# The attention's streamed output projection in another order of products, the last head's steps pinned, and a surcharge on POOL's DMAs in the FFN

## The chip, the core and the metric

The kernel runs on one core of a Trainium2 chip. A core has a matrix engine (PE), a vector engine (DVE), a scalar engine (ACT), a general engine (POOL) and an engine that issues DMAs (SP); each works through a queue of its own in order, and semaphores order them against each other. The metric is the device time of one execution in microseconds, over several runs; one further execution is recorded by the hardware profiler, and its rows are quoted below. PE = matmuls, PEld = weight loads; L73 is a helper line on which most vector operations are recorded, so groups are told apart by the tiles that they write and read.

## The reference

One decoder block in float32, sequence and model width 1024: a mixer, then cross-attention to 256 memory tokens, then a gated FFN of width 2816, each behind an rmsnorm and with a residual, and a last rmsnorm. What the change touches:

```python
def mem_cross_attention(n, m, w_xq, w_xkv, w_xo):
    q = (n @ w_xq).reshape(Bsz, S, 4, 256)
    k, v = jnp.split(m @ w_xkv, 2, axis=-1)
    ...
    p = jax.nn.softmax(s, axis=-1)
    o = jnp.einsum('bhsm,bmhd->bshd', p, v).reshape(Bsz, S, 1024)
    return o @ w_xo

def swiglu(n, w_ffn_in, w_ffn_out):
    g, u = jnp.split(n @ w_ffn_in, 2, axis=-1)
    return (jax.nn.silu(g) * u) @ w_ffn_out
...
h = h + mem_cross_attention(rmsnorm(h), rmsnorm(mem), w_xq, w_xkv, w_xo)
h = h + swiglu(rmsnorm(h), w_ffn_in, w_ffn_out)
```

## The kernel before

Every large product is done by seven block products instead of eight (Strassen in Winograd's form). Their names are those of the right operand: B11, B21 and B22 are blocks as they are, T1 to T4 are sums of blocks. Each operand in float32 is split into a high half (a copy on ACT, L233, into a rounded type) and a low half (a subtraction on DVE, L73), and three matmuls, high with high, high with low, low with high, stand for one (L51). So each product needs an ACT step, a DVE step and, for the sums, more steps on DVE or POOL before PE can begin it.

The stages that matter here follow each other:

1. The attention, class Att: for each of four heads h and two halves j of the rows a `score` (matmuls, then on DVE the maximum and the scaled negative of it, on ACT the exponentials, on DVE the reciprocal of the sum and the multiplication by it, tile pe), a `turn` (PE transposes pe; ACT and DVE split it, tile phl) and a `value` (matmuls, copied by ACT into the rows rq of the next product's right operand).
2. The output projection xo, an object of class Stored: its weights stream in (tiles wr; sums of weight blocks were prepared by POOL's DMAs in the DRAM tensor xos_d), both operands are split (tiles ws), products are taken in the order SEQ, and DVE adds them into tiles wk and ga that hold the residual. A block of the output that is final goes through post_xo: stored to h2_d by SP, scaled by ACT into the rows of the FFN's right operand, and its squares summed for the norm (tiles sq, ssum).
3. The FFN: eleven pairs of Units, gate and up, of 256 columns each. Their right operands are an object of class Operands, B, which `upto` brings on step by step. A Unit's weights (tile raw) are summed on POOL or DVE into sa and, for T3 and B22, in place (raw<-raw, raw<-raw,sa), split into whi and wlo, and used. Outputs are tiles o; gpost multiplies a gate's block by the norm (ssum), applies the silu and multiplies again; upost multiplies gate by up and forms the sums of blocks that the down projection takes, and SP stores them in act_d.
4. Beside the FFN, weight_sums issues DMAs on POOL that build the sums of the down projection's weights in down_d, some of them accumulating.

The order on each engine is not written out. A scheduler orders the instructions by times that it estimates; `ahead` gives priority, and `pinned` keeps an instruction in program order with the others that are pinned. `either(ap)` gives an operation to POOL or DVE, whichever of two meters (DVE.t, POOL.t), which add up estimated durations, says would end it sooner. Slots ("op", "aux", "m", "ga") are pools of buffers; a tile may not be written before its slot's last reader is through.

Of the kernel before, what the change touches and what calls it, by code (L numbers as in the profile page):

```python
# [13 lines left out]
ALU = mybir.AluOpType  # L14
AX = mybir.AxisListType
# [63 lines left out]
def block_kernel(ctx: ExitStack, tc: tile.TileContext, t: dict, out: bass.AP):  # L79
# [398 lines left out]
    def store_rows(dst, func=None):  # L478
# [6 lines left out]
            return post  # L485
        return mk

    def weight_sums(todo):


        jobs = []
        for A, d, n, k0 in todo:
            put = lambda m, d=d, n=n, k0=k0, kn=A.shape[2]: (
                d[(m * n + k0) * P:(m * n + k0 + kn) * P].rearrange("(k p) c -> p k c", p=P))
            q = {(i, j): A[j][:, :, half(i)] for i in range(2) for j in range(2)}
            jobs.append([(put(0), q[1, 0], 0), (put(2), q[0, 0], 0), (put(0), q[1, 1], 1), (put(2), q[1, 0], 1),
                         (put(1), put(0), 0), (put(3), q[0, 1], 0), (put(1), q[0, 0], 1), (put(3), put(1), 1)])
        for step in zip(*jobs):
            for o, a, more in step:
                kn = o.shape[1]  # L500
                for c in (slice(0, kn // 2), slice(kn // 2, kn)) if more and kn > 3 else (slice(0, kn),):
                    if more:
                        pinned(POOL.dma_start(o[:, c], a[:, c], accum_op=ALU.add))
                    else:
                        pinned(POOL.dma_start(o, a))
                    yield

    def w_in_units(c0, n, mk):
# [721 lines left out]
    class Wide:  # L1230
# [59 lines left out]
        def fetch(s, m, kp):  # L1290
# [8 lines left out]
            if x == 5:  # L1299
                s.load("T4")  # L1300

        def prep(s, n, pin=None):
            pin = pin or (lambda x: x)
            while len(s.ops) < min(n, 14):
                m, kp = divmod(len(s.ops), 2)
                name, c = s.SEQ[m], slice(2 * kp, 2 * kp + 2)
                s.load(name)
                x = [slot("op", (P, 2, 2, HALF), F32R, name="ws") for _ in range(2)]
                with ahead():
                    if name in s.COMB:  # L1310
                        f, *q = s.COMB[name]
                        o, a, b = (s.quad(*ij)[:, c] for ij in q)
                        f(DVE, o, a, b)
                    split(s.raw[name][:, c], x[0][:, 0], x[0][:, 1], pin=pin)
                    split(s.quad(*s.RIGHT[name])[:, c], x[1][:, 0], x[1][:, 1], neg=name == "T2", pin=pin)
                if name in ("T1", "T2") and s.PLUS:
                    s.raw[s.SEQ[m + 1]] = s.raw[name]
                    s.plus(s.SEQ[m + 1], 2 * kp)
                s.ops.append(x)

        def evac(s, name, u, p):
            i, j = s.OUT[name]
# [39 lines left out]
    class Stored(Wide):  # L1362
# [13 lines left out]

        def fetch(s, m, kp):
            s.load(*s.SEQ[:m + 3])
            if s.base is not None:
                for ij in {0: ((0, 0), (1, 1)), 2: ((0, 1),), 8: ((1, 0),)}.get(2 * m + kp, ()):  # L1380
                    s.home(*ij)

    class Left:

# [224 lines left out]
    def post_xo(o, h, q, last):  # L1609
# [1 line left out]
        ACT.activation(row_xo(o)[:, half(h)], q, AF.Copy, scale=col("norm_ffn", o))  # L1611
        u_xo_stats.take(h, q)

    xo = Stored(t["w_xo"], post_xo, {"T2": "aux", "B21": "aux", "*": "m"},
                {(0, 0): "m", (1, 1): "aux", (0, 1): "aux", (1, 0): "ga"}, h1_d)
    xo.sums_d = xos_d

    class Att:


        def __init__(s, h, j):
            s.h, s.j = h, j

        def score(s, a2):
            kvh, kvl = kv[s.h][:, 0], kv[s.h][:, 1]
            q = [i_q[2 * s.h + i][:, :, half(s.j)] for i in range(2)]
            if s.j == 1 and a2 == 0:
                pe[s.h] = slot("aux", (P, 2, 4, 256), name="pe")
            s.e = pe[s.h][:, s.j]
            p = acc()  # L1630
            for a in range(2):
                o = p[:, a * 256:(a + 1) * 256]
                c = slice((2 * a2 + a) * P, (2 * a2 + a + 1) * P)
                m = 0
                for i in range(2):
                    for x, y in ((0, kvh), (1, kvh), (0, kvl)):
                        PE.matmul(o, q[i][:, x, c], y[:, i], start=m == 0, stop=m == 5)
                        m += 1
            pv = p.rearrange("p (a m) -> p a m", m=256)
            mx = cp.tile([P, 2], F32, name="mx", tag="mx", bufs=3)  # L1640
            DVE.tensor_reduce(mx, pv, AX.X, ALU.max)
            c0 = 4 * s.j + 2 * a2
            DVE.scalar_tensor_tensor(mx, mx, -1.0, xsc[:, c0:c0 + 2], ALU.mult, ALU.mult)
            sm = cp.tile([P, 2], F32, name="sm", tag="sm", bufs=3)
            for a in range(2):
                ACT.activation(s.e[:, 2 * a2 + a], pv[:, a], AF.Exp, bias=mx[:, a:a + 1],
                               scale=xsc[:, c0 + a:c0 + a + 1], accum_out=sm[:, a:a + 1])
            DVE.reciprocal(sm, sm)
            for a in range(2):
                DVE.tensor_scalar(s.e[:, 2 * a2 + a], s.e[:, 2 * a2 + a], sm[:, a:a + 1], None, ALU.mult)  # L1650

        def turn(s, a2):
            if a2 == 0:
                s.pT = [bank(), bank()]
            for a in range(2):
                c = 2 * a2 + a
                for i in range(2):
                    PE.transpose(s.pT[i][:, c * P:(c + 1) * P], s.e[:, c, i * P:(i + 1) * P], ident)
            if a2 == 1:
                s.p = slot("aux", (P, 2, 2, HALF), F32R, name="phl")  # L1660
                for i in range(2):
                    split(s.pT[i], s.p[:, 0, i], s.p[:, 1, i])

        def value(s):
            kvh, kvl, ph, pl_ = kv[s.h][:, 0], kv[s.h][:, 1], s.p[:, 0], s.p[:, 1]
# [7 lines left out]
                ACT.activation(xo.rows(2 * s.h + i, s.j), p, AF.Copy)  # L1673

    pe = {}
    at = [Att(h, j) for h in range(4) for j in (1, 0)]
    for n in range(len(at) + 2):
        a = at[n] if n < len(at) else None
        b = at[n - 1] if 0 < n <= len(at) else None
        z = at[n - 2] if n > 1 else None  # L1680
        if a and a.j == 1 and a.h < 3:
            load_kv(a.h + 1)
        if a:
            a.score(0)
        if b:
            b.turn(0)
        if z:
            z.value()
        if b:
            b.turn(1)  # L1690
        if a:
            a.score(1)
        if n in (3, 4):
            xo.load(xo.SEQ[n - 3])
        if n in (7, 8):
            xo.prep(n - 6)
# [4 lines left out]
    for u in range(D_FF // 256):  # L1701
# [35 lines left out]
        if u < 2:  # L1737
            gate.e = up.e = DVE
        gu.append([gate, up])
    B = Operands(lambda: Row(row_xo), 4, swap=1, order=("B11", "T1", "B21", "B22", "T2", "T3", "T4"))  # L1740
    for n, _ in enumerate(xo.steps()):
        if n >= 8:
            B.upto(2 * n - 14)
        if n == 11:
            gu[0][0].load()
        if n == 13:
# [128 lines left out]
                          stop=k0 + k == KP - 1 and m == 2, skip_group_check=True)  # L1875

    run(group(gu[0], B, gu[1], order=B.order), (side, 1.0))
    w_down = t["w_ffn_out"].rearrange("(k j p) c -> j p k c", j=2, p=P)
    last_sums = chain(weight_sums([(w_down[:, :, k:min(k + 3, KP)], down_d, KP, k)]) for k in range(0, KP, 3))
    for u in range(1, len(gu)):  # L1880
# [79 lines left out]
```

## Time and profile before

| What | Value |
|---|---|
| runs, us | 1949.55, 1950.52, 1953.47 |
| median of the runs, us | 1950.52 |
| the profiled execution, us | 1952.81 |
| its span, from first to last instruction, us | 1951.1 |
| mean granted PE clock | 0.991 |
| POOL in the profile: busy us, instructions | 538.4, 432 |
| DVE: busy us, instructions | 1383.3, 1962 |
| end of the attention, projection, first FFN pairs | about 1100 to 1420 us of the span |

A row of the timeline has the start, the duration, the engine, the line, the operation, the tiles out<-in with partitions and elements, and how many equal ones follow each other; in brackets is how long the engine was idle just before, and what ended that wait ("issue": nothing that the profile shows). A row of the windows has the busy time of each engine in a stretch. A wait costs time only if the engine that waits is the one that the end depends on.

### The profile page before, as it was taken

How to read it: one execution, taken by the hardware profiler on the slowest of the kernel's cores; microseconds unless marked ns; L12 is line 12 of the kernel's file. 1: busy time of each engine (PE TensorE's matmuls, PEld its weight loads, DVE VectorE, ACT ScalarE, POOL GpSimd, SP SyncE). 2: the span in 40 equal slices, each digit the busy share in tenths (PEclk: the TensorE clock that was granted, in tenths of full speed). 3: DMA queues.
4: the chain of work that ended last, by engine and by line, in shares of the span. 5: the costliest groups of instructions: out<-in, count | busy, mean ns of one | idle time of the engine just before them, and what ended most of it. 6: DMA issues, size and time to landing. Idle time of an engine off the chain costs nothing. (4 is left out here: it accounts for less than half of the span.)

```text
span 1951.1 us, 26054 instructions
## 1 busy us (share of the span) xinstructions
PE 1894.7 (97%) x9632; PEld 1592.5 (82%) x9632; DVE 1383.3 (71%) x1962; ACT 901.3 (46%) x1541; POOL 538.4 (28%) x432
## 2 busy tenths in 40 slices
PE   7999999999999999999999998989799999999998
PEld 7998787888878888788888896878688788888888
DVE  7765879877776764653578777887577777866566
ACT  7534564655543544642247565653233333345243
POOL 0012334345443221001112110235444444330002
PEclk9999999999999999999999998999899999999999
DMA  9433383446563653988665563426565555387463
GB/s 345 139 93 101 130 307 108 155 160 191 167 184 122 198 159 119 363 310 247 169 173 201 145 155 126 137 80 173 146 188 158 145 158 167 89 290 272 161 223 125
DMA packets 242899, 345.23 MB, mean 177 GB/s; under 512 B 16442, under 2 KB 143652, under 8 KB 242772
## 3 DMA queue, kind: packets, MB, share of 16 engines
q1 hardware_dynamic: 223380, 293.23, 44.1%
q0 software_dynamic: 17664, 44.04, 10.8%
q10 hardware_dynamic: 1728, 6.29, 0.8%
q8 instruction: 76, 1.25, 0.3%
q14 instruction: 51, 0.42, 0.1%
HBM read 254.06 MB, written 129.30 MB: 196 GB/s over the span
## 5 line engine op out<-in xcount | busy, mean ns | idle before, releaser
L73 DVE TENSOR_TENSOR wlo<-raw,whi 128x512 fp32r<-128x512 f32 x272 | 241.6, 896 | 95.0 <-ACT whi L233 94.9
L233 ACT ACTIVATE whi<-raw 128x512 fp32r<-128x512 f32 x272 | 169.2, 629 | 243.5 <-PE acc L51 204.3
L73 DVE TENSOR_TENSOR o<-acc,o 128x512 f32<-128x512 f32 x244 | 166.9, 684 | 87.6 <-PE acc L51 84.8
L51 PE MATMUL acc<-hl,wd 128*128 128x512 f32 x768 | 174.7, 389 | 1.5 <-ACT wd L233 1.1
L51 PEld LDWEIGHTS acc<-hl,wd 128*128 128x128 f32 x768 | 143.9, 188 | 32.3 <-ACT wd L233 1.7
L51 PE MATMUL acc<-fs 128*128 128x512 f32 (+1 forms) x792 | 155.7, 355 | 0.1
L51 PEld LDWEIGHTS acc<-fs 128*128 128x128 f32 x792 | 130.7, 189 | 20.7 <-issue 0.5
L51 PE MATMUL acc<-ws 128*128 128x512 f32 x576 | 133.9, 390 | 1.4 <-DVE wk L73 1.1
L51 PEld LDWEIGHTS acc<-ws 128*128 128x128 f32 x576 | 107.7, 188 | 24.5 <-issue 1.5
L73 DVE TENSOR_TENSOR fs<-fr,fs 128x1024 fp32r<-128x1024 f32 (+1 forms) x78 | 93.4, 1225 | 35.8 <-ACT fs L233 35.1
L233 ACT ACTIVATE fs<-fr 128x1024 fp32r<-128x1024 f32 (+1 forms) x78 | 74.5, 984 | 92.0 <-PE bank L51 28.7
L233 ACT ACTIVATE whi<-sa 128x512 fp32r<-128x512 f32 x96 | 59.7, 627 | 99.9 <-PE acc L51 98.7
L51 PE MATMUL bank<-ws 128*128 128x512 f32 x432 | 99.8, 390 | 0.0
L73 POOL TENSOR_TENSOR sa<-raw 128x512 f32<-128x512 f32 x43 | 66.6, 1550 | 119.2 <-DMA raw<-in_w_in_dram 73.5
L73 POOL TENSOR_TENSOR raw<-raw,sa 128x512 f32<-128x512 f32 x35 | 45.4, 1298 | 194.3 <-DVE wlo L73 194.3
L51 PEld LDWEIGHTS bank<-ws 128*128 128x128 f32 x432 | 81.4, 188 | 17.0
L73 POOL TENSOR_TENSOR ssum<-ssum,sq 128x512 f32<-128x512 f32 (+1 forms) x24 | 38.2, 1591 | 196.9 <-ACT sq L525 184.4
L73 DVE TENSOR_TENSOR o<-o,ssum 128x512 f32<-128x512 f32 x67 | 65.9, 984 | 35.4 <-ACT o L1704 34.1
L51 PE MATMUL acc<-T1h,whi 128*128 128x512 f32 x192 | 77.6, 404 | 11.3 <-ACT whi L233 8.7
L51 PE MATMUL acc<-T4h,whi 128*128 128x512 f32 x192 | 76.7, 400 | 2.1 <-DVE o L73 2.0
L51 PE MATMUL acc<-B21h,wlo 128*128 128x512 f32 x192 | 76.3, 399 | 2.3 <-DVE wlo L73 2.3
L51 PE MATMUL acc<-T1h,wlo 128*128 128x512 f32 x192 | 76.4, 398 | 1.9 <-DVE wlo L73 1.9
(421 smaller groups left out, 5110.1 us busy)
## 6 DMA issues: line engine op xcount, KB each, us to landing
raw<-in_w_in_dram SPq DMA_DIRECT2D x26, 1024.0 KB, 5.8
raw<-in_w_ffn_in_dram SPq DMA_DIRECT2D x22, 1024.0 KB, 6.7
act_d<-o SPq DMA_DIRECT2D x77, 256.0 KB, 3.7
fr<-act_d SPq DMA_DIRECT2D x35, 512.0 KB, 5.9
down_d<-in_w_ffn_out_dram POOLq DMA_DIRECT2D x18, 768.0 KB, 7.4
fr<-down_d SPq DMA_DIRECT2D x20, 512.0 KB, 3.8
csb<-cs_d SPq DMA_DIRECT2D x15, 512.0 KB, 4.3
fr<-in_w_ffn_out_dram SPq DMA_DIRECT2D x15, 512.0 KB, 6.7
```

The source lines that it names most:

```text
L51: return s.e.matmul(o, x, y, **kw)
L73: return f(*a, **kw)
L233: pin(ACT.activation(hi, src, AF.Copy))
```

## The change

It has four parts. In the attention the halves are taken in the order (0, 1) instead of (1, 0), and the DVE steps of the last head, h = 3, are pinned. The projection becomes a Kept: its products stand in the order B11, B21, T1, T2, B22, T3, T4 instead of B11, T1, B22, T2, B21, T3, T4; the splits of B21 and T1 (steps 2 to 5) are pinned; all its weights come from one pool of slots; its residual tiles are fetched at other steps; the combination for T3 is made early. FFN operands: B no longer swaps the two column halves and is brought on from the projection's fourth step, B11 first. And once the first FFN pair is done, each DMA step of weight_sums adds 3.0 to POOL's meter.

```diff
+    slower = [0.0]
+
     def weight_sums(todo):
...
                     else:
                         pinned(POOL.dma_start(o, a))
+                    POOL.t += slower[0]
                     yield
...
     run(group(gu[0], B, gu[1], order=B.order), (side, 1.0))
+    slower[0] = 3.0
...
+                at = pin or (pinned if len(s.ops) in s.pins else free)
...
+    class Kept(Stored):
+
+        SEQ, FIRST, pins = Wide.SEQ, Wide.FIRST, (2, 3, 4, 5)
+
+        def fetch(s, m, kp):
+            x = 2 * m + kp
+            s.load(*s.SEQ[:m + 3])
+            for ij in {0: ((0, 0),), 2: ((1, 1),), 4: ((0, 1),), 8: ((1, 0),)}.get(x, ()):
+                s.home(*ij)
+            if x == 5:
+                for c in (slice(0, 2), slice(2, 4)):
+                    s.combine("T3", c, lambda x: x)
+                s.combined = ("T3",)
...
-    xo = Stored(t["w_xo"], post_xo, {"T2": "aux", "B21": "aux", "*": "m"},
-                {(0, 0): "m", (1, 1): "aux", (0, 1): "aux", (1, 0): "ga"}, h1_d)
+    xo = Kept(t["w_xo"], post_xo, {"*": "m"},
+              {(0, 0): "m", (1, 1): "aux", (0, 1): "aux", (1, 0): "ga"}, h1_d)
...
+            s.pin = pinned if h == 3 else lambda x: x
...
-            DVE.tensor_reduce(mx, pv, AX.X, ALU.max)
+            s.pin(DVE.tensor_reduce(mx, pv, AX.X, ALU.max))
...
-                    split(s.pT[i], s.p[:, 0, i], s.p[:, 1, i])
+                    split(s.pT[i], s.p[:, 0, i], s.p[:, 1, i], pin=s.pin)
...
-    at = [Att(h, j) for h in range(4) for j in (1, 0)]
+    at = [Att(h, j) for h in range(4) for j in (0, 1)]
...
-    B = Operands(lambda: Row(row_xo), 4, swap=1, order=("B11", "T1", "B21", "B22", "T2", "T3", "T4"))
+    B = Operands(lambda: Row(row_xo), 4, order=("B11", "T1", "B21", "B22", "T2", "T3", "T4"))
     for n, _ in enumerate(xo.steps()):
-        if n >= 8:
-            B.upto(2 * n - 14)
+        if n >= 4:
+            B.upto(min(n - 3, 4) if n < 10 else min(2 * n - 14, 8))
```

What this does to the order on the engines is seen at three places. The first is DVE at the end of the attention, where the last score's sum is inverted (sm), the probabilities are normalized (pe) and their low half is made (phl), while products of the projection are evacuated (wk) and its operands split (ws) or summed (rq). Before:

```order
L73 RECIPROCAL sm_10490<-sm_10490 128x2
L73 SCALAR_TENSOR_TENSOR wk_10561<-acc_10556,wk_10561 128x512
L73 SCALAR_TENSOR_TENSOR wk_10561<-acc_10557,wk_10561 128x512
L73 TENSOR_TENSOR rq_10138<-rq_10379,rq_10138 128x1024
L73 TENSOR_TENSOR ws_10597<-rq_10138,ws_10597 128x1024
L73 TENSOR_SCALAR pe_10343<-pe_10343,sm_10490 128x256 x2
L73 TENSOR_TENSOR ws_10639<-wr_10559,ws_10639 128x1024
L73 SCALAR_TENSOR_TENSOR wk_10561<-acc_10558,wk_10561 128x512
L73 TENSOR_TENSOR ws_10640<-rq_10379,ws_10640 128x1024
```

and behind these four more of 128x1024 before phl. After, on the same engine at the same place:

```order
L73 RECIPROCAL sm_10490<-sm_10490 128x2
L73 TENSOR_SCALAR pe_10343<-pe_10343,sm_10490 128x256
L73 SCALAR_TENSOR_TENSOR wk_10561<-acc_10556,wk_10561 128x512
L73 TENSOR_SCALAR pe_10343<-pe_10343,sm_10490 128x256
L73 SCALAR_TENSOR_TENSOR wk_10561<-acc_10557,wk_10561 128x512
L73 TENSOR_TENSOR phl_10528<-bank_10502,phl_10528 128x512
L73 TENSOR_TENSOR phl_10528<-bank_10503,phl_10528 128x512
L73 SCALAR_TENSOR_TENSOR wk_10561<-acc_10558,wk_10561 128x512
L73 TENSOR_TENSOR rq_10062<-rq_10062,rq_10138 128x1024
```

All sums and splits of 128x1024 now stand behind phl. The second place is POOL in the second FFN pair (o_11514 and o_11518 are that pair's gate output before and after; raw_11800 and raw_11801 the up weights of the pair behind it). Before:

```order
L73 TENSOR_TENSOR o_11514<-o_11514,ssum_9902 128x512
L73 DMA down_d_83<-in_w_ffn_out_dram 128x3x512
L73 TENSOR_TENSOR o_11514<-o_11514,ssum_9902 128x512
L73 DMA down_d_83<-in_w_ffn_out_dram 128x3x512 x2
L73 DMA down_d_83<-down_d_83 128x3x512
L73 TENSOR_TENSOR sa_11975<-raw_11800 128x512
L73 TENSOR_TENSOR sa_11977<-sa_11975,raw_11800 128x512
L73 TENSOR_TENSOR raw_11800<-raw_11800 128x4x128
```

After, on POOL at the same place:

```order
L73 TENSOR_TENSOR o_11518<-o_11518,ssum_9902 128x512
L73 DMA down_d_83<-in_w_ffn_out_dram 128x3x512 x3
L73 DMA down_d_83<-down_d_83 128x3x512
L73 TENSOR_TENSOR sa_11975<-raw_11801 128x512
L73 TENSOR_TENSOR sa_11977<-sa_11975,raw_11801 128x512
L73 DMA down_d_83<-in_w_ffn_out_dram 128x3x512
```

The last row of before, the T3 step on the weights, and one multiplication have left POOL; the four DMAs stand ahead of the sum sa as they did. The third place is DVE in the same pair, at the splits wlo of the up unit's T3, B22 and T4 weights (raw_11513) and the evacuations of its products (o<-acc). After, DVE has:

```order
L73 TENSOR_TENSOR wlo_11746<-raw_11513,whi_11745 128x512
L73 TENSOR_TENSOR o_11664<-acc_11709,o_11664 128x512
L73 TENSOR_TENSOR wlo_11766<-raw_11513,whi_11765 128x512
L73 TENSOR_TENSOR raw_11801<-raw_11801 128x4x128
L73 TENSOR_TENSOR wlo_11785<-raw_11513,whi_11784 128x512
L73 TENSOR_TENSOR o_11518<-o_11518,o_11664 128x512
L73 TENSOR_TENSOR o_11664<-acc_11691,o_11664 128x512
```

The same rows stood there before, but for the fourth: the T3 step on the next pair's up weights has come to DVE, between the splits for B22 and for T4.

More of the change, by code (lines that the diff above doesn't have):

```diff
@@ L1300, in fetch @@
                 s.load("T4")
+        pins = ()
+        combined = ()
         def prep(s, n, pin=None):
-            pin = pin or (lambda x: x)
+            free = lambda x: x
             while len(s.ops) < min(n, 14):
@@ L1309, in prep @@
                 with ahead():
[L1310 to L1315, printed above, removed]
+                    if name in s.COMB and name not in s.combined:
+                        s.combine(name, c, at if s.pins else free)
+                    split(s.raw[name][:, c], x[0][:, 0], x[0][:, 1], pin=at)
+                    split(s.quad(*s.RIGHT[name])[:, c], x[1][:, 0], x[1][:, 1], neg=name == "T2", pin=at)
                 if name in ("T1", "T2") and s.PLUS:
@@ L1319, in prep, with combine @@
                 s.ops.append(x)
+        def combine(s, name, c, pin):
+            f, *q = s.COMB[name]
+            o, a, b = (s.quad(*ij)[:, c] for ij in q)
+            pin(f(DVE, o, a, b))
         def evac(s, name, u, p):
@@ L1378, in fetch @@
             s.load(*s.SEQ[:m + 3])
-            if s.base is not None:
-                for ij in {0: ((0, 0), (1, 1)), 2: ((0, 1),), 8: ((1, 0),)}.get(2 * m + kp, ()):
-                    s.home(*ij)
+    class Kept(Stored):
[9 more added lines that the diff above has]
+                s.combined = ("T3",)
     class Left:
@@ L1626, in score @@
             q = [i_q[2 * s.h + i][:, :, half(s.j)] for i in range(2)]
-            if s.j == 1 and a2 == 0:
+            if s.j == 0 and a2 == 0:
                 pe[s.h] = slot("aux", (P, 2, 4, 256), name="pe")
@@ L1640, in score @@
             mx = cp.tile([P, 2], F32, name="mx", tag="mx", bufs=3)
-            DVE.tensor_reduce(mx, pv, AX.X, ALU.max)
+            s.pin(DVE.tensor_reduce(mx, pv, AX.X, ALU.max))
             c0 = 4 * s.j + 2 * a2
-            DVE.scalar_tensor_tensor(mx, mx, -1.0, xsc[:, c0:c0 + 2], ALU.mult, ALU.mult)
+            s.pin(DVE.scalar_tensor_tensor(mx, mx, -1.0, xsc[:, c0:c0 + 2], ALU.mult, ALU.mult))
             sm = cp.tile([P, 2], F32, name="sm", tag="sm", bufs=3)
@@ L1647, in score @@
                                scale=xsc[:, c0 + a:c0 + a + 1], accum_out=sm[:, a:a + 1])
-            DVE.reciprocal(sm, sm)
+            s.pin(DVE.reciprocal(sm, sm))
             for a in range(2):
-                DVE.tensor_scalar(s.e[:, 2 * a2 + a], s.e[:, 2 * a2 + a], sm[:, a:a + 1], None, ALU.mult)
+                s.pin(DVE.tensor_scalar(s.e[:, 2 * a2 + a], s.e[:, 2 * a2 + a], sm[:, a:a + 1], None, ALU.mult))
         def turn(s, a2):
@@ L1680, in block_kernel @@
         z = at[n - 2] if n > 1 else None
-        if a and a.j == 1 and a.h < 3:
+        if a and a.j == 0 and a.h < 3:
             load_kv(a.h + 1)
```

## The prediction

> **What bounds the kernel now.** I read the page's engine table first, then windows over the stretch that the change touches, then PE's waits there, and last the rows of single engines around each wait. A windows row has start and end, length, then busy time and (instructions) of PE, PEld, DVE, ACT, POOL, the granted clock, the DMA share and GB/s.
>
> ```profile
> PE 1894.7 (97%) x9632; PEld 1592.5 (82%) x9632; DVE 1383.3 (71%) x1962; ACT 901.3 (46%) x1541; POOL 538.4 (28%) x432
> ```
>
> ```profile
> 1190.00:1210.00 20.00, 12.68 (x46) 9.29 (x45) 15.68 (x18) 8.15 (x11) 0.00 (x0) 0.74 0.39 126
> 1250.00:1300.00 50.00, 43.35 (x179) 33.92 (x177) 49.65 (x74) 33.02 (x58) 13.87 (x10) 0.93 0.35 117
> 1350.00:1400.00 50.00, 39.71 (x166) 31.68 (x165) 27.71 (x36) 12.88 (x22) 20.02 (x16) 0.92 0.65 161
> 1390.00:1410.00 20.00, 13.74 (x48) 10.68 (x49) 11.49 (x15) 5.69 (x10) 9.58 (x7) 0.74 0.41 88
> 1500.00:1600.00 100.00, 97.76 (x426) 79.00 (x425) 75.16 (x95) 33.83 (x59) 47.37 (x36) 1.00 0.57 153
> 1600.00:1650.00 50.00, 50.00 (x222) 41.28 (x221) 39.80 (x51) 16.67 (x29) 22.35 (x16) 1.00 0.49 137
> 1165.10:1301.90 136.80, 122.48 (x538) 98.58 (x537) 117.43 (x162) 80.93 (x131) 19.30 (x12) 0.94 0.38 131
> ```
>
> PE sets the time: 97% of the span. At full rate it starts 222 matmuls in 50 us (row 1600), 4.44 a microsecond, and no edit removes a matmul. So the change is worth only what it takes from the few places where PE falls short. There are three large ones. **A**, the end of the attention: 46 matmuls in 20 us where 88.8 would fit, 9.6 us lost. **B**, the hand-over from output projection to FFN: of 179 in row 1250, 16 are short ones that take 2.5 us, and the other 163 need 36.7 us, so 10.8 us are lost. **C**, the second FFN pair: 56 missing in row 1350, 12.6 us, and some 0.8 just behind it. Row 1500 lacks another 2.2 us of PE time. What ends each wait stands in PE's rows, in brackets, in the parts below.
>
> **A, the pinned steps of the last head and the new second product.** First DVE's rows there, then PE's, then ACT's.
>
> ```profile
> 1190.99 1.22 DVE L73 TENSOR_TENSOR ws<-rq,ws 128x1024 fp32r<-128x1024 f32 x1
> 1192.13 0.61 DVE L73 TENSOR_SCALAR pe<-pe,sm 128x256 f32<-128x256 f32 x2
> ```
>
> ```profile
> 1192.53 0.70 PE L55 MATMUL bank<-ident,pe 128*128 128x128 f32 x4 [1.83 <-DVE pe L73]
> 1193.80 2.08 PE L51 MATMUL bank<-phl,kvhl 128*128 128x512 f32 x4 [0.58 <-ACT phl L233]
> 1200.80 2.93 PE L51 MATMUL bank<-phl,kvhl 128*128 128x512 f32 x6 [4.92 <-DVE phl L73]
> 1203.52 2.66 PE L51 MATMUL bank<-ws 128*128 128x512 f32 x10
> ```
>
> ```profile
> 1190.79 1.06 ACT L1673 ACTIVATE rq<-bank 128x512 f32<-128x512 f32 x2
> 1191.89 1.06 ACT L233 ACTIVATE ws<-rq 128x1024 fp32r<-128x1024 f32 x1
> ```
>
> The lost time is 1.83 + 0.58 + 4.92 = 7.3 us of waits and some 2.3 us of matmuls at the lower clock (0.74 in row 1190). DVE was never idle there: weight splits of 1.22 us, recorded "ahead", stood in front of the normalization (1192.13) and of the low half of the probabilities, phl, for which PE stood until 1200.80. Now these steps stand in program order and the splits behind them, so the waits for pe and phl go. 1203.5 less 7.3 and less 2.0 of the lower clock (the rest of it comes later) is 1194.2: there the attention's last value product would end. **What is late next:** the second product is B21, whose right operand is the output of the last heads. On ACT its splits stand behind the two copies of the last value product: 1.06 for these two, then two splits of 1.06, so 3.1 us of waiting, and 0.4 more for DVE's low half. The projection's second product starts near 1197.7 instead of 1203.5. The gain is 5.8 if the clock falls as it does now, and up to 6.5 if it holds; I take 5.5, with 3 as the lower end (DVE's backlog of splits moves behind and delays the evacuations) and 9.6, all of A, as the upper.
>
> [...]
>
> **B, the projection's order and the FFN's operands.** The stored summed weights are no longer needed second, the B11 operand of the FFN is split during the projection, and its first output block is final after two products instead of five. But B21 of the FFN now needs the projection's last product, which makes its split late. PE's rows:
>
> ```profile
> 1270.85 0.39 PE L51 MATMUL acc<-B11h,whi 128*128 128x512 f32 x1
> ...
> 1276.79 0.47 PE L51 MATMUL acc<-T1h,whi 128*128 128x512 f32 x1 [2.60 <-DVE ga L73]
> ...
> 1299.06 0.50 PE L51 MATMUL acc<-B22h,whi 128*128 128x512 f32 x1 [1.21 <-ACT whi L233]
> ```
>
> From 1270.85, 288 matmuls take 64.9 us, so with a start at 1197.7 the projection would end near 1262.6, 8 us sooner. Yet row 1250 has DVE at 49.65 of 50 us: DVE sets this hand-over, and it has nearly the same list (159 instructions against 162 in the last windows row). Behind the evacuation that frees the first FFN bank there now stand 24 DVE instructions at some 0.6 us ahead of the split for T1's second half, 14.6 us; PE has 77 matmuls, 17 us, in the same time, and each sum that POOL runs beside adds about 1 us to DVE. So waits like those for ga and whi (2.60, 1.21) return under other names. A and B have a common ceiling: DVE idles 136.8 − 117.4 = 19.4 us in the whole stretch. Their common floor is 0 (DVE gives back all that PE gained). I take 8 for both: A's 5.5 and 2.5, DVE then being busy 117 of 129 us.
>
> **C, POOL's load in the FFN.** A surcharge of 3 on each down-weight DMA moves 38 instructions from POOL to DVE: 18 T3 steps (raw<-raw), 11 multiplications by ssum, 8 operand sums, one sum of squares. POOL's rows around the stall, then DVE's, then PE's:
>
> ```profile
> 1338.58 0.80 POOL L73 DMA_DIRECT2D down_d<-in_w_ffn_out_dram  x1
> 1341.91 1.66 POOL L73 TENSOR_TENSOR o<-o,ssum 128x512 f32<-128x512 f32 x1 [2.54 <-DVE o L73]
> 1343.91 1.33 POOL L73 DMA_DIRECT2D down_d<-in_w_ffn_out_dram  x1 [0.34 <-issue]
> 1353.51 1.23 POOL L73 DMA_DIRECT2D down_d<-in_w_ffn_out_dram  x1 [8.27 <-issue]
> 1361.49 0.77 POOL L73 DMA_DIRECT2D down_d<-down_d  x1 [6.75 <-issue]
> 1362.28 1.29 POOL L73 TENSOR_TENSOR sa<-raw 128x512 f32<-128x512 f32 x1
> ...
> 1392.31 1.24 POOL L73 DMA_DIRECT2D down_d<-down_d  x1 [6.84 <-issue]
> 1393.10 1.74 POOL L73 TENSOR_TENSOR o<-o,ssum 128x512 f32<-128x512 f32 x1
> ```
>
> ```profile
> 1353.57 0.69 DVE L73 TENSOR_TENSOR wlo<-raw,whi 128x512 fp32r<-128x512 f32 x1 [1.93 <-ACT whi L233]
> ...
> 1362.29 1.84 DVE L73 TENSOR_TENSOR wlo<-sa,whi 128x512 fp32r<-128x512 f32 x1
> ```
>
> ```profile
> 1358.77 0.39 PE L51 MATMUL acc<-T4h,whi 128*128 128x512 f32 x1
> ...
> 1372.07 0.50 PE L51 MATMUL acc<-B21h,wlo 128*128 128x512 f32 x1 [2.27 <-DVE wlo L73]
> ...
> 1396.07 0.80 PE L51 MATMUL acc<-T1h,whi 128*128 128x512 f32 x1 [7.84 <-ACT whi L233]
> ```
>
> C was 2.27 + 7.84 and about 2.9 of lower clock behind the second (row 1390: 9.2 us short, of which 6.25 are waits), 13 in all. The 7.84 go: the multiplication at 1393.10, held behind two DMAs, is now DVE's. So do the 2.27. **But a new wait comes in their place.** The T3 step of the up weights two units on is now DVE's and stands in its queue just ahead of the split of T4 (1353.57), and it may not overwrite raw before POOL's sum sa<-raw has read it, at 1362.28, behind the four DMAs, which issue as before (the third and fourth held for 8.27 and 6.75 us). Behind the waiting DVE instruction stand T4's split, a product and the evacuation whose bank T4 uses; PE waits for them from 1358.77. The sum ends at 1363.6; then four steps at 0.6 spacing, the first perhaps 1.8 as POOL runs its second sum beside it (1362.29 shows that): T4 starts at 1366.4 to 1367.5, a wait of 7.6 to 8.7. With 2.9 of lower clock that is 11.0, and C gains 2.2. Were the longer hold of 8.27 as short as the one of 6.84, C would gain 3.6; were it a microsecond longer, with a wait like the 2.27 left behind it, C would lose 1.
>
> **The rest.** Row 1500's waits (2.2 us of PE) have the same cause as the one at 1393.10; I count 1.5 of it. The 38 moved instructions cost DVE 38 × 0.6 = 23 us over ten pairs; PE covers them at 40 of 50 us DVE load (row 1600), 43 with them. Were that cover gone, the price would be all 23; I count 0.5, since DVE's own waits in that row are longer than what is added. Loads of q, rows and weights on SP are the same number, only in another order.
>
> A POOL operation beside a DVE one costs DVE time now: 1.84 against 0.69 for the same shape. [...]
>
> Sum: 5.5 + 2.5 + 2.2 + 1.0 = 11.2 us from the profiled execution's 1952.8 (span 1951.1): 1941.6. That execution is 2.3 above the median of the runs shown, 1950.5; so 1939 on the scale of the median.
>
> **The rivals.**
> - *DVE gives A back.* In B DVE is full (49.65 of 50), so what PE gains at the attention's end it waits for at the hand-over: A + B = 0, and 3.2 are left, 1947. For it: that row. Against: DVE's 19.4 idle us in the stretch.
> - *The T3 step holds DVE in every pair (slower).* The step waits for the next gate's weights and POOL's first sum of them, and the split for B22 stands behind it:
>
> ```profile
> 1499.26 1.29 POOL L73 TENSOR_TENSOR sa<-raw 128x512 f32<-128x512 f32 x1 [4.74 <-DMA raw<-in_w_ffn_in_dram]
> ```
>
> ```profile
> 1503.48 0.39 PE L51 MATMUL acc<-B22h,wlo 128*128 128x512 f32 x1
> ```
>
>   The sum ends at 1500.55; T3 step 0.69 to 1.84 and split 0.68 put B22's split at 1501.9 to 1503.1, PE wants it at 1503.48: a margin of 0.4 to 1.6 us. SP now has the load behind one store more. Each microsecond beyond the margin costs PE one in nine gates; from 1.7 beyond it (15.1 / 9) the kernel is measurably slower. At 2 us: 18 lost, 1957. Against it: the store added ahead of the load is of T2, which comes early in the new order.
> - *The surcharge frees POOL as meant, C goes wholly.* If the DMAs no longer stand between, C gives 13 instead of 2.2: 1928. Against it: POOL's order, in which the four DMAs still stand ahead of the sum.
>
> **How the numbers follow.** Forecast 0.66 (1931 to 1946); DVE gives A back 0.14; T3 holds every pair 0.12; C goes wholly 0.08. A measurement of this kernel can tell about 0.2%, 3.9 us, from no change. Faster: forecast and the last, 0.74; within: 0.14; slower: 0.12. The range reaches from 1930 to 1950: the sum with C at 3.6, A + B at 15 (four fifths of their ceiling) and the rest at 2 is 1930, with C at −1 and A + B at 1.5 and the rest at nothing, 1950; outside are the slower rival and the last one.
>
> **What would show it.** In the changed profile: no wait for pe or phl over 1 us; one of about 3 us for ACT ws before the second product; DVE still full for 40 us around the hand-over; one wait of about 8 us at T4 of the second up unit, put down to a DVE row, with DVE itself waiting for POOL sa; no wait for whi at T1 of the pair behind it. Wrong would be: waits at B22 of each gate, or a clock below 1.00 in windows past 1410.

## The result, and the profile after

The changed kernel takes 1939.74 us (median of four runs, 1939.38 to 1940.62) against 1950.6 for the kernel before on the same chip: a ratio of 0.9943, with a 95% interval of 0.9925 to 0.996. The forecast was 1939.0. The profiled execution after took 1940.62, its span 1938.6, so 12.5 us less than the span before (10.9 between the medians); the sum had said 11.2.

The engine table and the windows of the changed kernel (columns as in the prediction: start and end, length, busy time and instructions of PE, PEld, DVE, ACT, POOL, granted clock, DMA share, GB/s):

```profile
PE 1890.6 (98%) x9632; PEld 1591.7 (82%) x9632; DVE 1377.1 (71%) x2000; ACT 900.7 (46%) x1541; POOL 491.0 (25%) x394
```

```profile
1190.00:1210.00 20.00, 16.91 (x67) 13.24 (x66) 18.91 (x19) 12.32 (x15) 0.00 (x0) 0.91 0.03 13
1250.00:1300.00 50.00, 44.60 (x198) 35.75 (x197) 50.00 (x76) 29.47 (x54) 18.40 (x8) 0.93 0.33 113
1300.00:1350.00 50.00, 48.26 (x215) 39.39 (x214) 33.42 (x43) 18.76 (x31) 25.29 (x19) 1.00 0.47 133
1350.00:1400.00 50.00, 42.91 (x178) 34.96 (x177) 34.05 (x49) 13.53 (x23) 17.23 (x13) 0.90 0.66 175
1600.00:1650.00 50.00, 50.00 (x220) 40.95 (x219) 35.93 (x52) 16.55 (x28) 15.42 (x11) 1.00 0.47 147
```

Row 1190 has 67 matmuls where it had 46. Row 1250 has DVE at 50.00 of 50: the hand-over is still DVE's. Row 1350 is little better than it was, 178 matmuls against 166. POOL has lost 38 instructions and DVE gained 38. PE's rows at the three places:

```profile
1196.21 1.20 PE L51 MATMUL bank<-ws 128*128 128x512 f32 x4 [2.84 <-ACT ws L233]
1197.66 11.74 PE L51 MATMUL bank<-ws 128*128 128x512 f32 x44 [0.25 <-DVE ws L73]
...
1275.61 0.52 PE L51 MATMUL acc<-B21h,whi 128*128 128x512 f32 x1 [2.35 <-ACT whi L233]
1279.27 0.79 PE L51 MATMUL acc<-T1h,wlo 128*128 128x512 f32 x1 [2.71 <-DVE wlo L73]
1321.53 0.50 PE L51 MATMUL acc<-T1h,wlo 128*128 128x512 f32 x1 [1.67 <-DVE wlo L73]
...
1359.22 0.80 PE L51 MATMUL acc<-T4h,whi 128*128 128x512 f32 x1 [7.09 <-DVE o L73]
```

The first wait is the one for ACT's split ahead of the second product, with a short one for DVE's low half four matmuls later. The next two are those of the hand-over under other names, the one at 1321.53 stands at T1 of the second gate unit, and the last is the new one at T4 of the second up unit. Behind it stands DVE, and behind DVE stands POOL:

```profile
1355.60 0.69 DVE L73 TENSOR_TENSOR raw<-raw 128x512 f32<-128x512 f32 x1 [10.75 <-POOL sa L73]
```

```profile
1338.21 1.31 POOL L73 DMA_DIRECT2D down_d<-in_w_ffn_out_dram  x1 [4.37 <-issue]
1345.75 1.24 POOL L73 DMA_DIRECT2D down_d<-in_w_ffn_out_dram  x1 [6.23 <-issue]
1353.52 0.76 POOL L73 DMA_DIRECT2D down_d<-down_d  x1 [6.54 <-issue]
1354.29 1.28 POOL L73 TENSOR_TENSOR sa<-raw 128x512 f32<-128x512 f32 x1
```

DVE did nothing for 10.75 us because its T3 step may not overwrite raw before POOL's sum, which stood behind held DMAs.

**Where the time went, by program points.** PE does the same matmuls in both kernels, so the same product can be looked up in two traces and its starts compared. This table is worked out from PE's timeline rows; each cell is the start in the profile before less the start in that kernel's profile, so time gained by then. The five points are the start of the FFN (before: 1270.85), T4 of the second gate unit (1339.27), of the second up unit (1358.77), of the third up unit (1410.55), and the end of the span (1951.1). "Time" is the median of the runs, the ratio is to the kernel before on the same chip, with its interval.

| kernel | time, us | ratio | FFN | gate 2 | up 2 | up 3 | end |
|---|---|---|---|---|---|---|---|
| the changed kernel | 1939.7 | 0.9943 (0.9925 to 0.996) | 7.2 | 6.4 | −0.5 | 10.5 | 12.5 |
| e1: no surcharge | 1929.1 | 0.9884 (0.9871 to 0.9898) | 8.0 | 6.7 | 6.5 | 20.2 | 23.7 |
| e2: before, surcharge alone | 1937.7 | 0.9933 (0.9921 to 0.9946) | −1.9 | 0.2 | 0.1 | 12.2 | 15.1 |
| e3: no pins | 1944.2 | 0.996 (0.9948 to 0.9973) | 2.0 | 2.6 | −4.3 | 7.3 | 7.9 |
| e8: before, pins alone | 1947.2 | 0.9981 (0.9971 to 0.9991) | 3.7 | 3.9 | 3.9 | 7.5 | 7.1 |
| e4: FFN operands later | 1942.2 | 0.9957 (0.9943 to 0.9971) | 7.3 | 1.2 | −6.0 | 5.1 | 8.1 |
| e6: T3 steps on POOL | 1928.6 | 0.9887 (0.9873 to 0.99) | 7.3 | 5.9 | 6.3 | 20.0 | 23.1 |
| e5: sums one pair later | 1930.0 | 0.989 (0.9876 to 0.9904) | 6.7 | 7.9 | 7.6 | 21.3 | 23.0 |
| e9: fewer DMAs ahead | 1937.6 | 0.9924 (0.9912 to 0.9936) | 7.3 | 6.0 | 6.5 | 20.2 | 17.2 |
| e10: e1, one DMA more ahead | 1932.7 | 0.9904 (0.989 to 0.9917) | 9.6 | 7.8 | 8.1 | 17.7 | 21.2 |
| e11: e1, up sums on POOL | 1930.0 | 0.9889 (0.9875 to 0.9902) | 6.3 | 6.6 | 6.9 | 19.8 | 23.3 |
| e12: e1, sums one pair later | 1929.7 | 0.9891 (0.9878 to 0.9905) | 7.6 | 8.5 | 8.0 | 21.7 | 23.1 |
| e13: e1, one copy on DVE | 1928.3 | 0.9885 (0.987 to 0.99) | 7.9 | 7.4 | 7.4 | 21.1 | 24.9 |

Six of these and the changed kernel have the same instruction order up to the FFN (e1, e5, e6, e9, e10, e12), and their first column runs from 6.7 to 9.6: single executions scatter by some 1.5 us to either side there, and smaller differences between columns of two kernels say nothing. One of e4's five runs took 2102.7 us at a granted clock of 0.848 (0.992 to 0.994 in the others); the ratio leaves it out, and without it the median is 1942.1.

For the changed kernel the table reads: 7.2 by the start of the FFN, 6.8 of it left just ahead of T4 of up 2 (the product in front of it starts at 1348.79 against 1355.59), the new stall there, yet the old stall behind it gone, so 3.7 more by up 3, and 2.0 in the rest.

### The profile page after: what moved, and what is told of

It is laid out like the page before. It is cut to its first block, busy times and chain, and to the rows that moved or that the text cites. A ratio compares the mean times of both kernels' runs of the same rounds, so it can differ in the third digit from the quotient of the medians.

```text
span 1938.6 us, 26040 instructions
## 1 busy us (share of the span) xinstructions
PE 1890.6 (98%) x9632; PEld 1591.7 (82%) x9632; DVE 1377.1 (71%) x2000; ACT 900.7 (46%) x1541; POOL 491.0 (25%) x394
## 4 chain that ended last, share of the span: by engine, by line
PE 83%; DVE 9%; issue 3%; DMA 2%; ACT 1%; POOL 1%; SPq 0%; POOLq 0%; DVEq 0%; ACTq 0%
PE acc L51 64%; PE bank L51 17%; DVE wlo L73 2%; DVE cv L73 2%; PE bank L55 2%; DVE o L73 1%; DMA raw<-in_w_ffn_in_dram 1%; DVE hs L73 1%; DMA hl<-ys_d 0%; POOL ssum L73 0%; DVE ws L73 0%; POOL o L73 0%; ACT cv L787 0%; DMA vraw<-in_w_in_dram 0%; DVE gy L73 0%
## 5 line engine op out<-in xcount | busy, mean ns | idle before, releaser
L73 DVE TENSOR_TENSOR wlo<-raw,whi 128x512 fp32r<-128x512 f32 x272 | 230.2, 855 | 85.8 <-ACT whi L233 85.7
L51 PE MATMUL acc<-B22h,wlo 128*128 128x512 f32 x192 | 76.0, 396 | 2.8 <-DVE wlo L73 2.8
L51 PE MATMUL acc<-B21h,whi 128*128 128x512 f32 x192 | 75.0, 391 | 2.3 <-ACT whi L233 2.3
```

Of the source, the lines that this page charges most:

```text
L51: return s.e.matmul(o, x, y, **kw)
L73: return f(*a, **kw)
```

## The experiments

**The surcharge, taken out and put in alone.** In e1 the changed kernel keeps its meter as it was; in e2 the kernel before gets the surcharge and nothing else.

```diff
-    slower[0] = 3.0
+    slower[0] = 0.0
```

> The changed kernel with the surcharge on the down-weight DMAs left at nothing: attention, projection and hand-over as changed, POOL's load in the FFN as before. Theory (the surcharge trades a stall of 13.7 us for one of 10.0 in the second pair and takes 2.0 us of small waits later, by the starts of the FFN products in the two traces): 3 to 6 us slower than the changed kernel, 1943 to 1946; the wait for DVE at T4 of the second up unit is gone, and waits for whi at T1 and for wlo at B21 of the pair behind it are back. Rival (the surcharge does nothing, the whole gain is from attention and hand-over): within 1 us of 1939.7, with waits of the same sum under other names.

> The kernel before with the surcharge of 3 added and nothing else. Theory: 3 to 6 us faster than before, 1944.5 to 1947.5, with one wait of 7 to 9 us at T4 of the second up unit put down to DVE, in place of the 2.27 and 7.84 behind it, and no wait over 1 us from 1430 on. Rival (surcharge and hand-over only pay together, since POOL's DMAs fall at another place of the pair when PE comes 7 us later): within 2 us of before, with waits at other places of the second or third pair.

Measured: e1 is not slower than the changed kernel but 10.6 us faster, 1929.1, with intervals that are far apart. e2 is 13.5 us faster than the kernel before, 1937.7, and has no wait at T4 of up 2. Neither the theory nor the rival of either run had its time. So the other edits alone are better than the two together, while the surcharge alone can't be told from both together: the intervals of e2 and of the changed kernel overlap. Row 1350 to 1400 of e1, then of e2, then POOL's rows of e1 and of e2 ahead of the sum:

```profile
1350.00:1400.00 50.00, 50.00 (x222) 41.42 (x221) 42.69 (x55) 16.12 (x27) 22.29 (x17) 1.00 0.68 192
```

```profile
1350.00:1400.00 50.00, 48.73 (x215) 39.88 (x214) 37.46 (x52) 15.89 (x27) 18.20 (x14) 1.00 0.60 163
```

```profile
1338.12 1.33 POOL L73 DMA_DIRECT2D down_d<-in_w_ffn_out_dram  x1 [0.21 <-issue]
1345.79 1.23 POOL L73 DMA_DIRECT2D down_d<-in_w_ffn_out_dram  x1 [6.34 <-issue]
1346.58 1.76 POOL L73 TENSOR_TENSOR sa<-raw 128x512 f32<-128x512 f32 x1
```

```profile
1343.02 1.31 POOL L73 DMA_DIRECT2D down_d<-in_w_ffn_out_dram  x1 [4.85 <-issue]
1350.80 1.23 POOL L73 DMA_DIRECT2D down_d<-in_w_ffn_out_dram  x1 [6.48 <-issue]
1351.60 1.76 POOL L73 TENSOR_TENSOR sa<-raw 128x512 f32<-128x512 f32 x1
```

The whole of C, 13.7 us by the table's columns up 2 and up 3 (20.2 less 6.5), is gone in e1, and 12.1 in e2. In both the copy down_d<-down_d no longer stands ahead of the sum, so there are three DMAs, not four, between the two pairs of sums. The sum starts 5.6 us (e1: 1346.58 against T4 at 1352.23) and 7.1 us (e2: 1351.60 against 1358.69) before PE comes to T4 of up 2. In the changed kernel, where PE was ready for T4 at 1351.96, it starts 2.3 us after that. The two halves of the change do not add up because both, by different ways, take away the same stall of the kernel before, and together they bring one of their own.

**What holds DVE: the T3 step.** Two kernels keep the surcharge and change what stands in that pair. e6 fixes the T3 steps to POOL; e5 asks for the down-weight DMAs one pair later.

```diff
-                sub(e, A21, A11, A21)
+                sub(s.e or POOL, A21, A11, A21)
```

```diff
-        run(group([gate], B, () if last else gu[u + 1][:1]), (last_sums, 0.4))
+        run(group([gate], B, () if last else gu[u + 1][:1]), (last_sums, 0.4 if u > 1 else 0.0))
...
-            if n == 2:
+            if n == 2 and u > 1:
```

> The changed kernel, surcharge and all, with every T3 step of the weights from the third pair on put on POOL instead of being left to the planner; by the planner's costs the sums ahead of them then go to DVE. Theory (the wait at T4 of the second up unit comes from DVE standing at a T3 step for POOL's sum): that wait of 7.1 and the 2.6 of lower clock behind it are gone though the four DMAs still stand together on POOL, 1928 to 1933. Rival (whatever stands behind the four DMAs on POOL holds PE, now the T3 step itself): a wait of 5 us or more at T3 or T4 of the third pair, 1935 to 1942.

> The changed kernel, surcharge and all, with the down-weight DMAs begun one pair later (none in the second pair; nothing else). Theory: no DMA stands ahead of POOL's sum for the T3 step of the second up unit, so its wait of 7.1 and the lower clock behind it go, and the first accumulating DMAs now fall in the third pair, where POOL's list has one or two between sums: 1928 to 1932. Rival (the three multiplications that now stand behind the first two DMAs, or the last DMAs, which come 38 us later, hold the gates as in the kernel before): 1935 to 1940.

Measured: 1928.6 and 1930.0, both as the theory had it. The window and POOL's rows of e6:

```profile
1350.00:1400.00 50.00, 50.00 (x222) 41.41 (x221) 38.97 (x59) 16.24 (x27) 15.16 (x12) 1.00 0.76 209
```

```profile
1345.91 1.24 POOL L73 DMA_DIRECT2D down_d<-in_w_ffn_out_dram  x1 [6.24 <-issue]
1354.19 0.76 POOL L73 DMA_DIRECT2D down_d<-down_d  x1 [7.05 <-issue]
1354.93 0.75 POOL L73 DMA_DIRECT2D down_d<-in_w_ffn_out_dram  x1
1355.70 1.30 POOL L73 TENSOR_TENSOR raw<-raw 128x512 f32<-128x512 f32 x1
```

The DMAs stand together and are held as long as in the changed kernel (6.24 and 7.05 us against 6.23 and 6.54), with one more behind them, and PE loses nothing: 222 matmuls in 50 us. What DVE's queue needs is no longer behind them (the planner, `either` with its meters, gave the two sums to DVE), and the T3 step itself, at 1355.70, is needed only late in the next pair. It isn't the DMAs that cost the 10 us but DVE's place behind them. e5's theory had the second pair free of DMAs, and three still stand there. But the two plain ones go at once, at 1329.71, and the accumulating one, at 1344.90, stands behind both of POOL's sums, so DVE's T3 step runs at 1346.03 without a wait.

**The number of DMAs, made less and more.** e9 asks the changed kernel's third gate for DMAs at 0.3 a product instead of 0.4; e10 asks e1's second gate at 0.6.

```diff
-(last_sums, 0.4)
+(last_sums, 0.3 if u == 2 else 0.4)
```

```diff
-(last_sums, 0.4)
+(last_sums, 0.6 if u == 1 else 0.4)
```

> The changed kernel, surcharge and all, but with the weight sums asked for a little less often in the third gate (0.3 a product instead of 0.4), so that three DMAs instead of four stand on POOL between the two pairs of sums for the third pair's weights; two sums, their copy and two more DMAs then stand together behind the last of them. Theory (what holds PE at T4 of the second up unit is the fourth DMA, held behind an accumulating one ahead of POOL's sum for the T3 step): that sum starts some 7 us sooner, the wait of 7.1 and the 2.6 of lower clock behind it go, up to 3 us come back where the DMAs now stand: 1929 to 1934. Rival (POOL has too much to do in that pair, whatever the order): the stall moves into the third pair, 1936 to 1942.

> The kernel without the surcharge (the one that took 1929.1), with the weight sums asked for more often in the second gate (0.6 a product instead of 0.4), so that four DMAs instead of three stand on POOL between the two pairs of sums for the third pair's weights. Theory (the count of DMAs at that place decides, not the surcharge): a stall of 7 us or more in the second or third pair, as in the kernel before, 1936 to 1944. Rival (the gain without the surcharge comes from POOL's other work, such as the T3 steps that stay on it): within 1.5 us of 1929.1.

e9 took 1937.6. The stall at up 2 is gone (20.2 by up 3), but not in the way that was meant: the planner moved up 3's sums to DVE, so again nothing of DVE's stood behind the DMAs. The rival's half came true as well: 5.4 us went in the pair behind it (by T4 of the gate after up 3 the gain was 14.8), and 1.8 more between up 9 and the end. Rows of PE, DVE and POOL there:

```profile
1410.72 0.79 PE L51 MATMUL acc<-B22h,wlo 128*128 128x512 f32 x1 [3.61 <-DVE wlo L73]
```

```profile
1408.31 0.69 DVE L73 TENSOR_TENSOR raw<-raw 128x512 f32<-128x512 f32 x1 [5.26 <-POOL sa L73]
```

```profile
1407.01 1.26 POOL L73 TENSOR_TENSOR sa<-raw 128x512 f32<-128x512 f32 x1 [9.74 <-DMA raw<-in_w_ffn_in_dram]
```

That is the prediction's second rival, the T3 step that holds DVE at a gate's B22, seen where the weights landed late.

e10 took 1932.7, 3.6 us more than e1; the theory had said 7 or more. Its window and POOL's rows:

```profile
1350.00:1400.00 50.00, 46.84 (x203) 37.49 (x202) 38.05 (x47) 14.93 (x26) 25.52 (x19) 1.00 0.67 169
```

```profile
1343.14 1.24 POOL L73 DMA_DIRECT2D down_d<-in_w_ffn_out_dram  x1 [6.29 <-issue]
1351.30 0.77 POOL L73 DMA_DIRECT2D down_d<-down_d  x1 [6.92 <-issue]
1352.09 1.30 POOL L73 TENSOR_TENSOR sa<-raw 128x512 f32<-128x512 f32 x1
```

The sum is as late as in the changed kernel (1.5 us after PE came to T4, at 1350.63), but here the T3 step is POOL's, DVE is not held, T4 does not wait, and only a string of waits of 0.4 to 1.3 us follows. By the table's columns up 2 and up 3, e10 gains 9.5 there where e1 gains 13.7. The intervals of the two ratios overlap, so the 4 us rest on the traces. So a late sum behind a fourth DMA costs some 4 us when POOL alone is late, and 10 when DVE stands behind POOL.

**The attention's end: pins and order apart.** e3 is the changed kernel without any pin; e8 is the kernel before with pins on the last head's steps and on the two splits of its second product (steps 2 and 3), in the old order.

```diff
-            s.pin = pinned if h == 3 else lambda x: x
+            s.pin = lambda x: x
...
-        SEQ, FIRST, pins = Wide.SEQ, Wide.FIRST, (2, 3, 4, 5)
+        SEQ, FIRST, pins = Wide.SEQ, Wide.FIRST, ()
```

> The changed kernel without program order for the last head's steps and for the splits of the projection's second and third products; the order of products, heads and FFN operands and the surcharge as changed. Theory (splits recorded ahead stand in DVE's queue before the normalization and the low half of the probabilities): waits for pe and phl of 5 to 8 us are back, the second product waits for its operands on top of them, and the kernel is 6 to 10 us slower than the changed one, 1946 to 1950. Rival (the order of products alone moves these splits back far enough): within 2 us of 1939.7, with waits for pe and phl under 1.5 us in all.

> The kernel before with program order for the steps of the last head and for the splits of the projection's second product, and nothing else: the stored sum is still the second product, the later products' splits and the combinations of right operands are still ahead. Theory (the pins by themselves bring A, since the second product there needs nothing of the last head): waits for pe and phl fall from 7.3 us to under 3, the second product starts 4 to 8 us sooner, and 3 to 6 us of it arrive at the end, 1944.5 to 1947.5. Rival (the splits held back are what the second product then waits for, and DVE's list is full at the hand-over): the second product starts within 2 us of 1203.5 or the hand-over gives it back, 1949 to 1952.

Measured: 1944.2 and 1947.2 (e8's eleven runs lie 10 us apart; its interval still ends below 1). By T4 of gate 2, e3 (order alone) has 2.6 us, e8 (pins alone) 3.9. Their sum, 6.5, is near what both have together, 6.4; with a scatter of 1.5 us for each, and with e8's pins on two splits instead of four, that it is so near is chance. PE's rows of e3, then of e8:

```profile
1195.38 2.08 PE L51 MATMUL bank<-phl,kvhl 128*128 128x512 f32 x4 [6.17 <-ACT phl L233]
1198.84 2.93 PE L51 MATMUL bank<-phl,kvhl 128*128 128x512 f32 x6 [1.38 <-DVE phl L73]
```

```profile
1191.43 3.02 PE L51 MATMUL bank<-phl,kvhl 128*128 128x512 f32 x12 [0.58 <-ACT phl L233]
1197.29 14.00 PE L51 MATMUL bank<-ws 128*128 128x512 f32 x48 [2.83 <-ACT ws L233]
```

Without pins the waits for phl are back (7.6 us), as the theory had it, but the second product doesn't wait on top of them, and 1.4 us of what is lost by the start of the FFN (5.2 against the changed kernel) is made up by gate 2: the time lies 2 us below the range given. The intervals of e3 and of the changed kernel just overlap, so here the rows are the evidence. With pins alone the second product starts at 1197.29, 6.2 us sooner, with the same wait for ws as in the changed kernel, although it needs nothing of the last head: ACT does its splits (the first at 1195.23) behind that head's two copies (1194.26, 1.08 us for both).

**The hand-over.** e4 asks for the FFN's B11 four steps later; e11 gives the first up unit's four weight sums to POOL; e13 puts one of the two copies on DVE (both of these on e1).

```diff
-        if n >= 4:
-            B.upto(min(n - 3, 4) if n < 10 else min(2 * n - 14, 8))
+        if n >= 8:
+            B.upto(min(n - 7, 4) if n < 12 else min(4 * n - 44, 8))
```

```diff
-            gate.e = up.e = DVE
+            gate.e, up.e = DVE, POOL if u == 0 else DVE
```

```diff
+                if (s.h, s.j, i) == (3, 1, 1):
+                    s.pin(DVE.tensor_copy(xo.rows(2 * s.h + i, s.j), p))
+                else:
                     ACT.activation(xo.rows(2 * s.h + i, s.j), p, AF.Copy)
```

> The changed kernel with the splits of the FFN's first operand, B11, asked for in the fifth product of the projection and later instead of in the third, and those of T1 correspondingly. Theory (DVE's list sets the hand-over, and the early splits fill no idle time, since DVE is full from 1200 on): the start of the second FFN pair moves by at most 1 us, 1938 to 1941. Rival (the early splits are what lets the FFN begin when the projection ends): a wait of 2 us or more at B11 or T1, 1942 to 1946.

> The kernel without the surcharge, with the four weight sums of the first up unit on POOL instead of DVE, at the hand-over, where DVE is full (20.00 of 20 us) and POOL is not (4.78). Theory (DVE's list sets the hand-over, and an operation of POOL beside it takes from DVE only part of what it spares): three of the four stand ahead of the late split, 0.6 us each, so 1 to 2 us faster, 1927 to 1928. [...]

> The kernel without the surcharge, with the second of the two copies of the last head's last value product on DVE instead of ACT. Theory (the wait of 2.84 us ahead of the projection's second product is these two copies of 1.06 each and a split of 1.06, one behind the other on ACT): it falls by about 1 us, to 1.8, and what DVE's list gives of it at the hand-over is under 1: 1928 to 1929.5. Rival (DVE's splits are as late as ACT's): no change of that wait.

e4: 5.2 us are lost by gate 2 (1.2 against 6.4) in the profiled execution, which took 1945.0; no single wait shows it, several of 0.4 to 3.1 do. The median is 1942.2, 2.5 us above the changed kernel, and the intervals overlap; the stall at T4 of up 2 is the same, 7.04. The theory, that a full DVE makes the early splits worthless, had at most 1 us at the second pair and does not hold there; how much they are worth lies between 2.5 and 5.

e11: 1930.0, no gain, where the theory had 1 to 2 us. The same four operations on DVE in e1 and in e11, then POOL's sums of the up unit in e11, then PE's longest wait there:

```profile
1259.62 2.48 DVE L73 TENSOR_TENSOR o<-o 128x512 f32<-128x512 f32 x4
```

```profile
1259.19 4.67 DVE L73 TENSOR_TENSOR o<-o 128x512 f32<-128x512 f32 x4
```

```profile
1260.10 1.53 POOL L73 TENSOR_TENSOR sa<-raw 128x512 f32<-128x512 f32 x1 [2.58 <-DMA raw<-in_w_ffn_in_dram]
1261.70 1.61 POOL L73 TENSOR_TENSOR sa<-sa,raw 128x512 f32<-128x512 f32 x1
1263.27 1.72 POOL L73 TENSOR_TENSOR raw<-raw 128x512 f32<-128x512 f32 x1
```

```profile
1279.53 0.79 PE L51 MATMUL acc<-T1h,wlo 128*128 128x512 f32 x1 [5.01 <-DVE wlo L73]
```

Three operations of 0.6 us left DVE's list, 1.8 us, and beside POOL's sums the four operations o<-o alone took 2.2 us longer: what was taken from DVE's list was paid by its other instructions. What makes them longer there was not shown.

e13: 1928.3, within the interval of e1. The wait for ACT's ws fell from 2.84 to 2.35, half of what was forecast: ACT's two copies took 1.08 us together in e1 (1192.67), not 1.06 each, so one fewer spared it 0.49. DVE did its copy at 1193.77, behind two sums of 2.47 us together.

**The DMAs asked for one pair later, without the surcharge.** e12 is e1 with e5's edit.

> The kernel without the surcharge, with the down-weight DMAs begun one pair later. Theory (without four DMAs ahead of a pair's sums nothing is left to gain in the second pair): within 1.5 us of 1929.1; the small waits after the sixth pair may go or come, 1 us. Rival (the accumulating DMAs cost DVE and PE something in each pair, and the pair that is now free of them shows it): 1925 to 1927.

1929.7: nothing left to gain there, as the theory had it. Two DMAs still stand in the second pair, at 1330.63 and 1346.22, so the rival, that a pair free of DMAs is faster, was not tried in full.

e1, e5, e6, e11, e12 and e13 all beat both kernels; against the kernel before they gain 20.9 to 22.3 us, and among themselves they can't be told apart. e1 is the simplest: the changed kernel without its surcharge.

## Why the prediction was right

The time (1939.0 against 1939.7) came out by the steps that the prediction named, but that it came out so near is luck: A gave 1.8 more than forecast, B 3.0 less, C 1.5 and the rest 1.0 more. Each was read from one execution, with some 1.5 us of scatter.

- **A.** Forecast 5.5; measured 7.3. The second product's first four matmuls start at 1196.21, the other 44 at 1197.66, where the kernel before starts its second product at 1203.52. The forecast of 1197.7 was for the first matmul, so its nearness to 1197.66 means nothing. The waits for pe and phl are gone, the one for ACT's ws is 2.84 (forecast 3.1), and the 0.25 for DVE (0.4) comes behind four matmuls, not ahead of them. e3, without the pins, has 7.6 us of waits for phl again.
- **A + B.** Forecast 8; 6.8 was left ahead of T4 of up 2. The FFN began at 1263.63 (forecast 1262.6), 7.2 us sooner, so B, which was to add 2.5, added nothing and cost 0.5 by up 2: it was the term sized worst. From its second product on, the projection took 67.4 us, not the 64.9 of the forecast. The clock behind the wait in A is hardly the reason: in e6 and e9 it held at 1.00, and their FFN began at 1263.52 and 1263.56. DVE was full, as said, and the other waits came back as 2.35 for whi and 2.71 for wlo, with a new one of 1.67 at 1321.53. By e4 the early B11 is worth 2.5 to 5 us; that it keeps the late last product from costing more was argued, not shown by itself.
- **C.** Forecast 2.2 (13 less 11); measured 3.7. The wait at T4 of up 2 was at the place, for the reason and nearly of the size that were given (7.09 against 7.6 to 8.7; the longest hold of a DMA ahead of that sum was 6.54, not 8.27, the case for which the prediction had 3.6), with 2.6 of lower clock behind it (0.50 from 1358 to 1362 and 0.66 from there to 1366; forecast 2.9), and neither of the two old waits was left. e6 and e5 confirm the cause: with the T3 step on POOL, or with the accumulating DMA behind the sums, it goes.
- **The rest.** Forecast 1.0, measured 2.0 (12.5 less 10.5). The waits of row 1500, 2.2 in all, went; in their place the 38 moved instructions cost PE one wait of 1.34.
- **The rivals.** DVE did not give back all of A. That the T3 step holds DVE at a gate's B22 is a real mechanism: in the changed kernel DVE waited nine times for POOL's sa ahead of a step on raw, 25.6 us in all, 10.75 of it at the stall. The view of the tile raw on DVE from 1340 to 1720 says so (us, then times):

```profile
its engine sat idle before it (us, times) until:
  POOL sa L73: 25.6, 9
```

Elsewhere PE did not notice, except for the 1.34 above, and in e9 it cost 3.61. That C goes wholly is what the surcharge does in the kernel before (e2), and what the other edits do without it (e1).

What the prediction didn't ask is what each part does without the other. It set the surcharge's stall against that of the kernel before and booked a gain; against the other edits alone the surcharge is a loss of 10.6 us. Why the scheduler puts the copy ahead of the sum with both edits and behind it with either was not isolated: it orders by estimated times, and all of its inputs in that pair move.

The list of what would show it held: no wait for pe or phl, one near 3 us for ACT's ws, DVE full at the hand-over, one long wait at T4 of up 2 with DVE waiting for POOL's sa, no wait for whi at T1 behind it, and from 1410 to 1920 the granted clock is 1.00. In A the clock fell (0.91 in row 1190), as the sum had taken it.

## What to carry to other kernels

When a change has several parts, put a sum of the kernel without each of them beside the sum against the kernel before: two parts may remove the same stall and pay for it twice. On an engine that takes its queue in order, ask of every instruction moved to it not what it lasts but what it waits for, and what stands behind it: a step of 0.69 us cost 10 us here, because it was moved to DVE while its releaser stayed behind DMAs on POOL. Ordering small work by a planner's estimate means that an edit of 0.1 in a rate moves other work across engines (e9), so read the order that was built before reading the time.

## What the runs showed of the hardware

Seven of the DMAs into down_d on POOL's queue stood directly behind an accumulating one in the changed kernel, and seven in the kernel before. Six of each were held ("issue" in brackets), for 6.21 to 7.46 us in the changed kernel and for 6.07 to 8.66 in the kernel before. The seventh waited 3.96 us (1654.91) and 3.91 (before, 1666.81). An accumulating one directly behind a plain one was held for 4.25 to 4.73 us in the changed kernel (three cases; 4.37 at 1338.21), and for 4.10 (e4) to 5.50 (e9) in the rows of other runs. In e1 a sum directly behind an accumulating one ran at once (issue at 1345.79, sum at 1346.58), and so did a plain DMA behind a plain one in e6 (1354.19 and 1354.93). What counted in these runs was so not the number of DMAs but whether something that is needed soon stood behind one that was held. What a held DMA waits for stays open: most rows name nothing, some the landing of a DMA before it (the changed kernel: the 3.96 at 1654.91; e10: 6.68 at 1383.26).

PE's clock at a wait of 2.84 us was not a matter of the wait's length alone. The wait ahead of the second product was 2.84 in the changed kernel and in e6, from one instruction order. Windows of the changed kernel, then of e6:

```profile
1190.00:1196.00 6.00, 3.37 (x15) 2.44 (x13) 4.91 (x6) 2.82 (x4) 0.00 (x0) 1.00 0.00 0
1196.00:1200.00 4.00, 3.54 (x10) 2.56 (x11) 4.00 (x5) 4.00 (x6) 0.00 (x0) 0.68 0.00 0
```

```profile
1190.00:1196.00 6.00, 3.77 (x17) 2.79 (x15) 4.90 (x7) 2.64 (x5) 0.00 (x0) 1.00 0.00 0
1196.00:1200.00 4.00, 3.15 (x12) 2.28 (x13) 4.00 (x4) 4.00 (x5) 0.00 (x0) 1.00 0.00 0
```

It fell to 0.68 in one and held at 1.00 in the other. Of the ten profiles with this wait of 2.84 or 2.83, it held at 1.00 in the row from 1196 in three (e6, e9, e10) and fell in seven, to 0.57 (e8, e11) to 0.77 (e5); after e13's 2.35 it fell too, to 0.57. Read in rows of 0.4 us, the changed kernel has 1.00 up to 1197.2, then one row at 0.82, 0.50 from 1197.6 to 1200.8, one row at 0.91, and 1.00 again: 3.4 us at 0.50. The rows of 1190 to 1204 of the other falls lack as much of the full clock, 1.70 to 1.72 us, and those of e8 3.40; if the clock was 0.50 there too, that is 3.4 us each and 6.8 in e8, an estimate from these rows. By the same reckoning the fall began 0.7 us before the wait's end in e8 (at 1196.56, the wait ending at 1197.29), 1.3 us behind it in the changed kernel and 2.0 us behind it in e12 (at 1197.6 against 1195.65). What decides whether and when it falls was not shown.
